# Taking GpSimd's tensor work in the mixing stages of a two-layer hybrid kernel over to VectorE and ScalarE

## The chip, the cores and the metric

The kernel runs on one core of a Trainium2 chip. The number that counts is the device time of one execution in microseconds (us). Three runs of the kernel before gave 1757.34, 1757.70 and 1763.57 us; their median is 1757.7 us.

A core has TensorE (PE in the profile, with its weight loads as PEld), VectorE (DVE), ScalarE (ACT), GpSimd (POOL) and SyncE (SP), which here only issues DMAs. Each engine works through its own queue in order; semaphores make one wait for another.

## The reference

Two layers work on 512 latent tokens and 256 context tokens of width 1024, all in float32. A layer mixes the tokens and then runs a gated MLP:

```python
mix_c, finals = token_mixers(modulate(cs, csh1, csc1), None, lw, want_out=not last, want_finals=True)
mix_x, _ = token_mixers(modulate(xs, sh1, sc1), finals, lw, want_out=True, want_finals=False)
xs = layer_norm(DEEPNORM_ALPHA * xs + g1 * mix_x, ln1_g[l], ln1_b[l])
ffn_x = conv_ffn(modulate(xs, sh2, sc2), ffn_w_up[l], ffn_conv_w[l], ffn_conv_b[l], ffn_w_down[l], rows)
xs = layer_norm(DEEPNORM_ALPHA * xs + g2 * ffn_x, ln2_g[l], ln2_b[l])
# token_mixers: proj = h @ w_in, and two groups on its columns
#   S5:  32 groups x 64 complex states, scanned forwards and backwards; y = Re(C states) + D u; gelu; glu
#   LRU: conv of 4, gates r, i; a = exp(-8 r softplus(-lam)); h = scan(a, sqrt(1-a^2) i x); (h_fwd + h_bwd) * gelu(g)
#   out = concat(y_s5, y_lru) @ w_out
```

The context tokens go through the same layers, except that the second layer needs only their final states.

## The kernel before

**Split products.** Every large matrix product is made of three passes at a reduced-precision format (`mm3`, lines 170 to 172). For it each operand is split into a high part and a low part: `split` (lines 158 to 163) writes `hi` as a rounded copy and `lo = src - hi`. `halves` (line 195) loads a piece of weights of 128 x 1024 into one of two staging buffers (`r0`, `r1`), and splits it; a staging buffer is free again when the low part is done. The high part is made by ScalarE (line 160), or, for `w_in` of the second layer, by GpSimd (line 162; `HIE = 'SG'`). The low part of all weights is made by GpSimd (line 163).

**Stages.** Each layer has a mixing stage and an FFN stage.

The mixing stage projects the normalised tokens with 12 column blocks of `w_in` (`proj`): u (S5 input), x (LRU input), g (LRU gate), four each. S5 works through eight head blocks `hb` of four groups. For each, `prep` gets two tables `ein` and `fo` (in the first layer from `outer`, lines 595 to 600, with `fo` on GpSimd and `ein` on VectorE; in the second from DRAM), transposes one, and makes a table of the products inside a block of 8 tokens. `enter` multiplies the inputs into states, copies them to SBUF and sets up `rt`, a broadcast of the decay (line 709, GpSimd). `leave` rotates by a table `cs` (lines 722 to 725), scans (line 727, twice), rotates back (731 to 738), multiplies out on TensorE (741 to 743), and ScalarE evicts the result (744). The rotation tables themselves come from `s5_params` (lines 575 to 577): for each `hb` three instructions on GpSimd for the cosine part, three on VectorE for the sine part. The first layer's are made inside its own mixing stage, the second layer's during the first layer's FFN stage. The LRU (`__call__`) makes gates with TensorE and ScalarE (783, 784), decays (794, 795, 803), scans on VectorE (804 to 812), and adds the two directions on GpSimd (line 813). After the last `hb`, `glu` loads the S5 result back from DRAM (961), applies gelu (965), splits it, multiplies by `w_glu`, gates it with a sigmoid (976, 977), and splits again; the LRU result, times its gelu gate (935), is split under the name `ylru` with its low part on GpSimd. Then come the products with `w_out`, the normalisation and the next features.

In the FFN stage (lines 1141 to 1180) TensorE runs nearly without a gap, VectorE does the convolution and GpSimd the low parts of the weights.

**Order.** The program is written in the order of its text, with priorities and filler work (matrix products for the modulation, `mods`) given in tables such as `FILL`; a scheduler with a timeline of its own then sets the order on each engine. Moving an instruction to another engine so changes the order of others as well.

Of the kernel before, what the change touches and what calls it, by code (L numbers as in the profile page):

```python
# [17 lines left out]
AF = mybir.ActivationFunctionType  # L18
ALU = mybir.AluOpType
MUL, ADD, SUB = ALU.mult, ALU.add, ALU.subtract  # L20
# [17 lines left out]
PI_LO = 3.1415925  # L38
PRIO = (300, 300)
PRIO2 = (0, 0)  # L40
HIE = 'SG'
VG = (1,)
PRIO3 = (0, 0)
MODS = (2, 1)
# [8 lines left out]
def body(ctx: ExitStack, tc: tile.TileContext, a, out):  # L53
    nc = tc.nc
    V, S, G, PE = nc.vector, nc.scalar, nc.gpsimd, nc.tensor
# [54 lines left out]
    def new(slot, shape, dt=F32):  # L110
        t, o, has = slots[slot]
        assert has == dt, (slot, dt)
        return carve(t, o, shape)
# [39 lines left out]
    V.memset(mhalf, -0.5)  # L153
    

    hi_eng = [None]

    def split(src, hi, lo, lo_eng):
        if hi_eng[0] is None:
            S.activation(hi, src, AF.Copy)  # L160
        else:
            hi_eng[0].tensor_scalar(hi, src, 1.0, None, op0=MUL)  # L162
        return lo_eng.tensor_tensor(lo, src, hi.bitcast(F32), op=SUB)  # L163
# [32 lines left out]
    def halves(src, hi, lo):  # L196

        raw = raws(hi.shape)
        with behind(hold[0]):
            weight_load[0] = load(raw, src)  # L200
        split(raw, hi, lo, G)
        return hi, lo


# [237 lines left out]
    def s5_params(l, scratch, raw_slots, phase_slots, cs_slots, tmp_slot, load=load):  # L442
# [27 lines left out]
        r8 = prm["r8"]  # L470
# [94 lines left out]
        for hb in range(8):  # L565
            yield
            step()
            gs = slice(4 * hb, 4 * hb + 4)
            cs = new(cs_slots[hb % 2], [128, 2, 4, 96])
            tt = new(tmp_slot, [128, 2, 4, 96])  # L570
            bh = lambda i: hi[:, i, gs].unsqueeze(3).to_broadcast([128, 4, 12, 8])
            bl = lambda i: lo[:, i, gs].unsqueeze(2).to_broadcast([128, 4, 12, 8])
            w = lambda x: x.rearrange("p g (a b) -> p g a b", b=8)
            for i, e, op in ((0, G, SUB), (1, V, ADD)):
                e.tensor_tensor(w(cs[:, i]), bh(0), bl(i), op=MUL)
                e.tensor_tensor(w(tt[:, i]), bh(1), bl(1 - i), op=MUL)
                e.tensor_tensor(cs[:, i], cs[:, i], tt[:, i], op=op)
            nc.sync.dma_start(csd[l, hb], cs.rearrange("p i g n -> p (i g n)"))
# [41 lines left out]
    class S5:  # L620
# [29 lines left out]
        def prep(self, hb):  # L650
# [4 lines left out]
            fo2 = fo.rearrange("p i g j c -> p i g (j c)")  # L655
            ein = new("a0", [128, 2, 4, 8, 16])
            if l == 0:
                outer(fo, hb, 2, prm["cc"], False, G, self.tg)
                outer(ein, hb, 0, prm["bb"], True, V, self.tv)
            else:  # L660
                load(ein.rearrange("p i g j c -> p (i g j c)"), tabd[hb, 0])
                load(fo.rearrange("p i g j c -> p (i g j c)"), tabd[hb, 1])
# [30 lines left out]
        def enter(self, hb, et):  # L693
# [12 lines left out]
            self.copy(v[0:64, :, :, 1:96], vv[0:64, :, :, 0:95])  # L706
            self.copy(v[64:128, :, :, 1:33], vv[64:128, :, :, 31::-1])
            self.copy(v[64:128, :, :, 33:96], vv[64:128, :, :, 95:32:-1])
            G.tensor_scalar(rt, self.prm["r8"][:, gs].unsqueeze(2).to_broadcast([128, 4, 96]), 1.0, None, op0=MUL)
            G.memset(rt[:, :, 0:1], 0.0)  # L710
            cs = new("t0", [128, 2, 4, 96])
            load(cs.rearrange("p i g n -> p (i g n)"), csd[self.l, hb])
# [34 lines left out]
    class LRU:  # L747
# [23 lines left out]
        def __call__(self, m, xc, bank):  # L771
# [33 lines left out]
            for d in range(2):  # L805
# [4 lines left out]
                    V.tensor_tensor_scan(h[:, 0:LAT], aa[:, 0:LAT], i_[:, 0:LAT], h[:, NT - 1:NT], op0=MUL, op1=ADD)  # L810
                else:
                    V.tensor_tensor_scan(h[:, ::-1], aa[:, ::-1], i_[:, ::-1], 0.0, op0=MUL, op1=ADD)
            G.tensor_tensor(hs[0][:, 0:keep], hs[0][:, 0:keep], hs[1][:, 0:keep], op=ADD)
            return hs[0]

    tmps = ring("gr", "gs")
# [53 lines left out]
    for l in range(DEPTH):  # L870
# [2 lines left out]
        ntok = 128 * nt  # L873
        order = order0[6 - nt:]
        cols, coef = par[l]
        if l > 0:
            mixing_phase()

# [142 lines left out]
        where[0] = f"ylru{l}"  # L1021
        ylru = [[new(f"h{2 * m + i}", [128, NT], F32R) for i in range(2)] for m in range(4)]
        for m in range(4):
            split(ge[0][:, m, 0:ntok], ylru[m][0][:, 0:ntok], ylru[m][1][:, 0:ntok], G)

        ys5 = y5s[0]
        phase("right", (F32R, several("x", 6, 4)), (F32R, {"w6": 4, "w7": 4}))
        where[0] = f"out{l}"
        gt = new("v", [128, 2, D])
        g1 = [bcast(gt[:, v], gd[l][0, v]) for v in range(1 if last else 2)]  # L1030
        xin = [new("u", [128, 3, D]), new("e", [128, 3, D])]
# [270 lines left out]
```

## Time and profile before

| | us |
|---|---|
| median of three runs | 1757.7 |
| the profiled execution | 1757.56 |
| its span, first to last instruction | 1755.8 |
| PE busy | 1562.5 (89%) |
| DVE busy | 1302.9 (74%) |
| POOL busy | 807.7 (46%) |
| ACT busy | 648.1 (37%) |

The stages can be told apart in the page's 40 slices of 43.9 us each: the first layer's mixing takes slices 1 to 8 and its FFN stage ends in the 23rd or 24th; the second layer's mixing ends in the 30th. An engine's busy time is the sum of the times from its instructions' starts to their ends, so a duration is read beside that of the same shape elsewhere. The stretch from 43.3 us (the modulation factors of the first features are done) to 299.7 us (the last S5 scan of the first layer ends) is called the head below, and that from there to 366.0 us (the last gate product of `glu`) the tail.

### The profile page before, as it was taken

What the parts mean: (1) busy time and instruction counts of PE and PEld (TensorE: products, weight loads), DVE (VectorE), ACT (ScalarE), POOL (GpSimd) and SP (SyncE); (2) the same over time, 40 slices, a digit from 0 to 9 for tenths busy, and PEclk for the clock granted to TensorE, in tenths of its full rate; (3) what the DMA queues carried; (4) which work ended last, traced back from release to release, by engine and by line L of the source; (5) the groups of instructions that cost most, each with busy time, mean ns of one, the idle gap of its engine ahead of it and who ended that gap; (6) DMA issues with size and microseconds to landing.
All of it is one profiled execution on the core that took longest, in us unless ns stands there. A gap on an engine that the chain in (4) does not pass through costs nothing. (4 is left out here: it accounts for less than half of the span.)

```text
span 1755.8 us, 22958 instructions
## 1 busy us (share of the span) xinstructions
PE 1562.5 (89%) x8824; PEld 1267.1 (72%) x8824; DVE 1302.9 (74%) x2104; ACT 648.1 (37%) x941; POOL 807.7 (46%) x496
## 2 busy tenths in 40 slices
PE   4768778898999999999999779989869899999996
PEld 1656655677888787887888658767547888888884
DVE  7999999478566995677689883889557476555587
ACT  2426445633633222222222136344661643323320
POOL 2567543548332244522325383533156454444474
PEclk8788898999899999999999898998879899999998
DMA  8335435742221212423334315665463333232231
GB/s 332 105 114 162 136 113 185 231 154 92 78 72 61 96 49 97 156 109 131 118 118 150 111 52 185 212 213 171 152 209 125 102 120 108 84 108 96 85 120 60
DMA packets 95359, 227.10 MB, mean 129 GB/s; under 512 B 28912, under 2 KB 39696, under 8 KB 95248
## 3 DMA queue, kind: packets, MB, share of 16 engines
q1 hardware_dynamic: 85456, 212.92, 36.3%
q10 hardware_dynamic: 9792, 12.71, 2.0%
q8 instruction: 69, 1.13, 0.3%
q14 instruction: 42, 0.34, 0.1%
HBM read 194.50 MB, written 31.10 MB: 128 GB/s over the span
## 5 line engine op out<-in xcount | busy, mean ns | idle before, releaser
L170 PE MATMUL banks<-ar,ar 128*128 128x512 f32 (+2 forms) x2152 | 777.6, 367 | 49.1 <-ACT ar L160 16.8
L171 PE MATMUL banks<-ar,ar 128*128 128x512 f32 (+2 forms) x2152 | 778.3, 363 | 17.3 <-DVE ar L396 7.8
L172 PE MATMUL banks<-ar,ar 128*128 128x512 f32 (+2 forms) x2152 | 770.9, 362 | 2.3 <-DVE ar L163 2.2
L163 POOL TENSOR_TENSOR ar<-ar,ar 128x1024 fp32r<-128x1024 f32 (+1 forms) x184 | 456.0, 2485 | 572.2 <-ACT ar L160 479.5
L170 PEld LDWEIGHTS banks<-ar,ar 128*128 128x128 f32 x2152 | 412.8, 193 | 134.0 <-ACT ar L160 20.8
L171 PEld LDWEIGHTS banks<-ar,ar 128*128 128x128 f32 x2152 | 415.7, 193 | 82.9 <-DVE ar L396 9.7
L172 PEld LDWEIGHTS banks<-ar,ar 128*128 128x128 f32 x2152 | 415.5, 193 | 65.7 <-DVE ar L163 4.2
L160 ACT ACTIVATE ar<-ar 128x1024 fp32r<-128x1024 f32 (+3 forms) x236 | 226.1, 976 | 496.7 <-PE banks L171 202.1
L1141 DVE SCALAR_TENSOR_TENSOR ar<-banks,cols,ar 128x441 f32<-128x441 f32 (+2 forms) x352 | 243.1, 691 | 41.8 <-ACT ar L1136 35.0
L1175 DVE TENSOR_TENSOR ar<-banks,ar 128x512 f32<-128x512 f32 x160 | 109.0, 685 | 117.4 <-PE banks L172 115.4
L163 DVE TENSOR_TENSOR ar<-ar,ar 128x512 fp32r<-128x512 f32 (+1 forms) x64 | 77.8, 1228 | 56.0 <-ACT ar L160 39.1
L826 POOL TENSOR_TENSOR ar<-ar 128x512 f32<-128x512 f32 x40 | 62.2, 1560 | 47.8 <-DVE ar L822 47.1
L1148 ACT ACTIVATE ar<-ar,cols 128x768 f32<-128x768 f32 (+1 forms) x44 | 36.6, 831 | 122.2 <-DVE ar L1141 71.4
L185 PE MATMUL banks<-ar,cond 128*32 128x256 f32 x192 | 64.8, 441 | 18.9 <-DMA ar<-in_w_mod_dram 18.9
L384 PE MATMUL banks<-ident,ar 128*128 128x128 f32 x176 | 36.5, 345 | 34.4 <-ACT ar L358 16.4
L188 PE MATMUL banks<-ar,cond 128*32 128x256 f32 x576 | 65.8, 441 | 0.0
L396 DVE TENSOR_TENSOR ar<-ar,ar 128x256 fp32r<-128x256 f32 (+1 forms) x64 | 41.4, 666 | 32.9 <-ACT ar L395 32.6
L783 PE MATMUL banks<-ar,ar 128*128 128x512 f32 (+1 forms) x128 | 54.7, 550 | 7.8 <-issue 6.9
L162 POOL TENSOR_SCALAR ar<-ar 128x1024 fp32r<-128x1024 f32 x12 | 35.5, 2958 | 49.2 <-PE banks L171 27.5
L384 PEld LDWEIGHTS banks<-ident,ar 128*128 128x128 f32 x176 | 26.2, 175 | 41.5 <-ACT ar L358 17.4
L1136 ACT ACTIVATE ar<-banks,cols 128x512 f32<-128x512 f32 x44 | 29.9, 679 | 69.7 <-PE banks L172 69.6
L185 PEld LDWEIGHTS banks<-ar,cond 128*32 128x32 f32 x192 | 15.8, 115 | 54.8 <-DMA ar<-in_w_mod_dram 32.4
(255 smaller groups left out, 1921.0 us busy)
## 6 DMA issues: line engine op xcount, KB each, us to landing
ar<-in_w_mod_dram SPq DMA_DIRECT2D x96, 512.0 KB
ar<-in_ffn_w_up_dram SPq DMA_DIRECT2D x88, 512.0 KB
ar<-in_ffn_w_down_dram SPq DMA_DIRECT2D x44, 512.0 KB
ar<-in_w_in_dram SPq DMA_DIRECT2D x24, 512.0 KB
tabd<-ar SPq DMA_DIRECT2D x16, 512.0 KB
ar<-tabd SPq DMA_DIRECT2D x16, 512.0 KB
csd<-ar SPq DMA_DIRECT2D x16, 384.0 KB
ar<-csd SPq DMA_DIRECT2D x16, 384.0 KB
```

The source lines that it names most:

```text
L160: S.activation(hi, src, AF.Copy)
L163: return lo_eng.tensor_tensor(lo, src, hi.bitcast(F32), op=SUB)
L170: PE.matmul(ps, wh, xh, start=first and k == 0, stop=False)
L171: PE.matmul(ps, wh, xl, start=False, stop=False)
L172: PE.matmul(ps, wl, xh, start=False, stop=last and k == nk - 1)
L185: ins = PE.matmul(*args, **kw)
L188: ins = PE.matmul(*args, **kw)
L384: PE.transpose(tp[:, o:o + 128], z[:, 128 * k:128 * k + 128], ident)
L783: PE.matmul(gp, w[:, d, i, :], xc[:, o:o + n], start=True, stop=True)
L826: G.tensor_tensor(xs_t[:, cs], xs_t[:, cs], tmp, op=ADD)
L1141: inst[0] = V.scalar_tensor_tensor(av[:, yo, xo], uv[:, yi, xi], tap(1 + dy, 1 + dx, ch), av[:, yo, xo], op0=MUL, op1=ADD)
L1175: V.tensor_tensor(acc, ps, acc, op=ADD)
```

## The change

`HIE` becomes `'SS'`: ScalarE makes the high parts of `w_in` in both layers. A variable `lo_eng` says who makes the low parts of weights: VectorE in the mixing stages (`w_in`, `w_glu`), GpSimd from the output product on (`w_out` and the FFN weights), as before. VectorE also takes the cosine half of the rotation tables of both layers, the table `fo` of the first layer, the sum of the two LRU directions and the low part of `ylru`; ScalarE takes the broadcast `rt`. What is left to GpSimd in the mixing stages are memsets and the small steps of the normalisation.

```diff
-HIE = 'SG'
+HIE = 'SS'
...
-    hi_eng = [None]
+    hi_eng, lo_eng = [None], [V]
...
             weight_load[0] = load(raw, src)
-        split(raw, hi, lo, G)
+        split(raw, hi, lo, lo_eng[0])
         return hi, lo
...
-            for i, e, op in ((0, G, SUB), (1, V, ADD)):
+            for i, e, op in ((0, V, SUB), (1, V, ADD)):
                 e.tensor_tensor(w(cs[:, i]), bh(0), bl(i), op=MUL)
...
             if l == 0:
-                outer(fo, hb, 2, prm["cc"], False, G, self.tg)
+                outer(fo, hb, 2, prm["cc"], False, V, self.tg)
                 outer(ein, hb, 0, prm["bb"], True, V, self.tv)
...
-            G.tensor_scalar(rt, self.prm["r8"][:, gs].unsqueeze(2).to_broadcast([128, 4, 96]), 1.0, None, op0=MUL)
+            S.activation(rt, self.prm["r8"][:, gs].unsqueeze(2).to_broadcast([128, 4, 96]), AF.Copy)
...
-            G.tensor_tensor(hs[0][:, 0:keep], hs[0][:, 0:keep], hs[1][:, 0:keep], op=ADD)
+            V.tensor_tensor(hs[0][:, 0:keep], hs[0][:, 0:keep], hs[1][:, 0:keep], op=ADD)
...
         cols, coef = par[l]
+        lo_eng[0] = V
         if l > 0:
             mixing_phase()
...
         for m in range(4):
-            split(ge[0][:, m, 0:ntok], ylru[m][0][:, 0:ntok], ylru[m][1][:, 0:ntok], G)
+            split(ge[0][:, m, 0:ntok], ylru[m][0][:, 0:ntok], ylru[m][1][:, 0:ntok], V)
...
         where[0] = f"out{l}"
+        lo_eng[0] = G
         gt = new("v", [128, 2, D])
```

In all, 140 instructions come to VectorE: 36 low parts (line 163: 24 of `w_in`, 4 of `w_glu`, 8 of `ylru`), 48 of lines 575 to 577, 48 of lines 595 to 600 and 8 of line 813; 28 come to ScalarE: 12 high parts and 16 of line 709. From line 876 on the new text's line numbers are one higher, from line 1023 on two.

The scheduler's order changes in three places that matter here. The first is VectorE at the end of the first layer's mixing. Before, after the last scan (727) and its rotation back, the last LRU part (798 and on) begins:

```order
L727 SCALAR_TENSOR_TENSOR ar_68<-ar_68 128x384 x2
L731 TENSOR_TENSOR ar_68<-ar_68 128x768
L732 TENSOR_TENSOR ar_68<-ar_68 128x768
L735 TENSOR_TENSOR ar_68<-ar_68 64x384
L737 TENSOR_TENSOR ar_68<-ar_68 64x4x32
L738 TENSOR_TENSOR ar_68<-ar_68 64x4x64
L735 TENSOR_TENSOR ar_68<-ar_68 64x384
L737 TENSOR_TENSOR ar_68<-ar_68 64x4x32
L738 TENSOR_TENSOR ar_68<-ar_68 64x4x64
L798 TENSOR_TENSOR ar_83<-ar_83,ar_87 128x768
```

Now the last LRU part (its scans 812 and 810, its sum 813), the last low part of `w_in` and the gate (936, line 935 before) stand ahead of that scan:

```order
L812 SCALAR_TENSOR_TENSOR ar_89<-ar_84,ar_85 128x768
L810 SCALAR_TENSOR_TENSOR ar_88<-ar_82,ar_88,ar_83 128x512
L722 TENSOR_TENSOR ar_68<-ar_68 128x768
L723 TENSOR_TENSOR ar_68<-ar_68 128x768
L813 TENSOR_TENSOR ar_88<-ar_88,ar_89 128x768
L163 TENSOR_TENSOR ar_67<-ar_68,ar_67 128x1024
L724 TENSOR_TENSOR ar_68<-ar_68 128x384
L725 TENSOR_TENSOR ar_68<-ar_68 128x384
L936 TENSOR_TENSOR ar_68<-ar_68,ar_80 128x768
L727 SCALAR_TENSOR_TENSOR ar_68<-ar_68 128x384 x2
L731 TENSOR_TENSOR ar_68<-ar_68 128x768
L732 TENSOR_TENSOR ar_68<-ar_68 128x768
```

So the whole last LRU part moved from behind the last S5 block to ahead of its scan.

The second place is ScalarE there, around the eviction of the last S5 block (744) and its store to DRAM (648). Before, they follow the last decay of the LRU (803) at once:

```order
L803 ACTIVATE ar_88<-ar_88,lru_st_2068 128x768
L803 ACTIVATE ar_89<-ar_89,lru_st_2068 128x768
L744 ACTIVATE ar_68<-banks 128x384
L648 DMA yd<-ar_68 128x768
L924 ACT_TABLE_LOAD
L924 ACTIVATE ar_68<-banks 128x512
```

Now the high parts of `ylru` (160, 128x768) and three of `w_out` (160, 128x1024 into `ar_66`) stand ahead of them:

```order
L160 ACTIVATE ar_66<-ar_68 128x768 x3
L160 ACTIVATE ar_66<-ar_68 128x1024 x2
L927 ACTIVATE ar_68<-banks 128x256
L160 ACTIVATE ar_66<-ar_68 128x768
L160 ACTIVATE ar_66<-ar_68 128x1024
L744 ACTIVATE ar_68<-banks 128x384
L648 DMA yd<-ar_68 128x768
```

The eviction moved behind other work of ScalarE, while the LRU's decays moved out of its way.

The third is GpSimd between the layers. Before, high and low parts of the second layer's `w_in` (162, 163) stand between the steps of the last normalisation (352, 366, 367), the residual sums (826) and the low parts of features (396):

```order
L396 TENSOR_TENSOR ar_66<-ar_68,ar_66 128x256
L162 TENSOR_SCALAR ar_67<-ar_68 128x1024
L826 TENSOR_TENSOR ar_68<-ar_68 128x512
L352 TENSOR_TENSOR ln_st_7506<-ln_st_7506,mhalf_98 128x1
L366 TENSOR_TENSOR ln_st_7467<-ln_st_7467,mhalf_98 128x1
L162 TENSOR_SCALAR ar_67<-ar_68 128x1024
L163 TENSOR_TENSOR ar_67<-ar_68,ar_67 128x1024
L704 MEMSET ar_68 128x8
L826 TENSOR_TENSOR ar_68<-ar_68 128x512
L704 MEMSET ar_68 128x8
L396 TENSOR_TENSOR ar_66<-ar_68,ar_66 128x256
```

Now none do:

```order
L396 TENSOR_TENSOR ar_66<-ar_68,ar_66 128x256
L826 TENSOR_TENSOR ar_68<-ar_68 128x512
L366 TENSOR_TENSOR ln_st_7467<-ln_st_7467,mhalf_98 128x1
L352 TENSOR_TENSOR ln_st_7506<-ln_st_7506,mhalf_98 128x1
L367 TENSOR_TENSOR ln_st_7467<-ln_st_7467 128x1
L704 MEMSET ar_68 128x8
L826 TENSOR_TENSOR ar_68<-ar_68 128x512
L704 MEMSET ar_68 128x8
L639 MEMSET ar_68 128x256
L396 TENSOR_TENSOR ar_66<-ar_68,ar_66 128x256
```

Three instructions of 128x1024 have left GpSimd's queue between these two steps of the features.

## Rows read from the trace of the kernel before

**Rows 1.** The page's 40 slices: busy tenths of DVE.

```profile
DVE  7999999478566995677689883889557476555587
```

**Rows 2.** By stretch: length; PE, PEld, DVE, ACT, POOL busy (count); PEclk; DMA; GB/s.

```profile
43.30:299.70 256.40, 195.76 (x1354) 154.91 (x1354) 249.85 (x374) 118.20 (x191) 149.14 (x105) 0.84 0.42 133
299.70:366.00 66.30, 57.00 (x341) 43.06 (x341) 39.81 (x37) 42.64 (x59) 32.00 (x13) 0.95 0.65 215
...
500.00:1006.00 506.00, 487.27 (x2637) 409.15 (x2635) 394.49 (x715) 125.39 (x153) 186.25 (x94) 0.99 0.31 106
1006.00:1066.00 60.00, 48.52 (x200) 37.61 (x201) 43.36 (x76) 26.28 (x49) 44.73 (x43) 0.81 0.26 95
1066.00:1255.00 189.00, 171.90 (x1314) 138.39 (x1313) 143.07 (x193) 88.28 (x149) 70.94 (x45) 0.91 0.61 192
1255.00:1316.00 61.00, 45.56 (x271) 31.35 (x270) 28.88 (x25) 39.70 (x54) 28.43 (x14) 0.80 0.54 177
```

**Rows 3.** Timeline, all engines, 83 to 91.5 us: start, duration, instruction, [idle before].

```profile
83.39 2.39 POOL L163 TENSOR_TENSOR ar<-ar,ar 128x1024 fp32r<-128x1024 f32 x1 [5.90 <-ACT ar L160]
83.44 2.50 DVE L261 TENSOR_TENSOR ar<-ar,ar 128x128 f32<-128x128 f32 x1
...
90.93 0.28 DVE L261 TENSOR_TENSOR ar<-ar,ar 128x128 f32<-128x128 f32 x1
```

**Rows 4.** DVE's groups by line and shape in the head: count, busy us, mean ns.

```profile
L723 DVE TENSOR_TENSOR ar<-ar 128x768 f32<-128x768 f32 x8 | 11.9, 1483 | 0.0
...
L597 DVE TENSOR_TENSOR ar<-ar,ar 128x512 f32<-128x512 f32 x8 | 9.3, 1168 | 0.0
...
L804 DVE SCALAR_TENSOR_TENSOR ar<-ar,ar 128x768 f32<-128x768 f32 x6 | 5.6, 938 | 0.0
L599 DVE TENSOR_TENSOR ar<-tab,bb 128x512 f32<-128x512 f32 x8 | 5.4, 678 | 0.0
```

**Rows 5.** POOL's groups by line and shape in the head.

```profile
L163 POOL TENSOR_TENSOR ar<-ar,ar 128x1024 fp32r<-128x1024 f32 x13 | 34.6, 2660 | 28.5 <-ACT ar L160 28.5
...
L709 POOL TENSOR_SCALAR ar<-r 128x384 f32<-128x384 f32 x7 | 14.1, 2021 | 23.0 <-DVE ar L727 23.0
```

**Rows 6.** Timeline of DVE, SP and ACT at the tail, 296 to 366 us.

```profile
296.60 0.54 DVE L724 TENSOR_TENSOR ar<-ar 128x384 f32<-128x384 f32 x1
297.07 0.55 DVE L725 TENSOR_TENSOR ar<-ar 128x384 f32<-128x384 f32 x1
...
303.61 0.42 DVE L738 TENSOR_TENSOR ar<-ar 64x256 f32<-64x256 f32 x1
...
313.09 0.47 ACT L744 ACTIVATE ar<-banks 128x384 f32<-128x384 f32 x1
...
324.34 0.20 ACT L963 ACTIVATE glu_st<-ar 128x1 f32<-128x1 f32 x1 [6.22 <-DMA ar<-yd]
...
339.85 3.15 DVE L163 TENSOR_TENSOR ar<-ar,ar 128x768 fp32r<-128x768 f32 x1
...
358.11 7.01 DVE L163 TENSOR_TENSOR ar<-ar,ar 128x512 fp32r<-128x512 f32 x6 [0.21 <-ACT ar L160]
```

**Rows 7.** Timeline between the layers, 1040 to 1056 us, all engines.

```profile
1046.06 2.77 POOL L162 TENSOR_SCALAR ar<-ar 128x1024 fp32r<-128x1024 f32 x1
...
1048.81 2.34 POOL L163 TENSOR_TENSOR ar<-ar,ar 128x1024 fp32r<-128x1024 f32 x1
...
1053.19 0.58 PE L171 MATMUL banks<-ar,ar 128*128 128x256 f32 x1 [6.11 <-POOL ar L396]
...
1053.49 1.28 DVE L830 SCALAR_TENSOR_TENSOR ar<-ar,ln_st 128x1024 f32<-128x1024 f32 x1
```

**Rows 8.** The whole run's groups by line and shape: ScalarE's high parts.

```profile
L160 ACT ACTIVATE ar<-ar 128x1024 fp32r<-128x1024 f32 x164 | 173.7, 1060 | 399.9 <-PE banks L171 139.4 <-DMA ar<-in_ffn_w_up_dram 96.2 <-PE banks L172 87.4
```

**Rows 9.** Timeline at the end of the second layer's mixing, 1284 to 1300 us.

```profile
1288.36 7.22 DVE L163 TENSOR_TENSOR ar<-ar,ar 128x512 fp32r<-128x512 f32 x3
...
1291.18 0.58 PE L171 MATMUL banks<-ar,ar 128*128 128x256 f32 x1 [2.17 <-DVE ar L163]
```

## The prediction

> **What bounds the kernel now.** I read the page's slices first. VectorE is at nine tenths or more in slices 2 to 7, that is, through the first layer's mixing, and again in a few slices of the FFN [rows 1]. The stretches then say what each stage hangs on [rows 2]. In the head (43.3 to 299.7 us) VectorE is busy 249.85 of 256.40 us, while TensorE is busy 195.76 and its clock stands at 0.84 of full, so part of it at the lower of its two levels (1.2 instead of 2.4 GHz): there VectorE is the bound. In the FFN stage (500 to 1006) TensorE is busy 487.27 of 506 us at 0.99. In the second layer's mixing (1066 to 1255) TensorE is busy 171.90 of 189 us, VectorE 143.07. Between them (1006 to 1066), in the tail (299.7 to 366) and at the end of the second mixing (1255 to 1316), nobody is full: chains of waits set the time.
>
> The timeline shows what VectorE's busy time is made of [rows 3]. GpSimd began a low part of 128x1024 at 83.39 and took 2.39 us; VectorE's product of 128x128, begun at 83.44, ended with it after 2.50 us. The same product took 0.28 us at 90.93. An instruction of VectorE with two operands in SBUF so stands until GpSimd is done. By lines and shapes [rows 4]: 128x768 takes 938 ns where it is undisturbed (line 804) and 1483 in the mean at line 723, which makes 8 x 0.545 = 4.4 us of waiting; 128x512 takes 678 (599) and 1168 (597), 3.9 us. The same subtraction over all 83 groups of VectorE in the head gives 79 us. GpSimd is busy 149.14 us there [rows 2], and it stands as well.
>
> **The change part by part.** *Head.* The 79 us of waiting go, as GpSimd keeps only memsets. What comes: by the new order, 87 moved instructions lie between the first modulation factors and the last scan: 13 low parts at 1.28 us (128x1024 on VectorE with two SBUF operands, line 830 [rows 7]), 46 of lines 595 to 600 at 0.678, 24 of lines 575 to 577 at 0.55 [rows 6], 4 sums at 0.938: 16.6 + 31.2 + 13.2 + 3.8 = 64.8 us. The last LRU part, which the scheduler takes ahead of the last scan, adds ten instructions, about 10.2 us (seven of 128x768 and three scans), and three moved ones before 43.3 us add 2.6. VectorE starts an instruction before the one ahead of it has ended: 0.47 us apart where each takes 0.55 [rows 6]. For 100 instructions at 0.07 that takes 7 off. VectorE's time is then 249.85 - 79 + 64.8 + 10.2 + 2.6 - 7 = 241.4 us, with the idle 6.55 as before 248, against 256.4: -8. Its inputs must be ready as often as now, though it no longer falls behind while it stands; I take -5. The ends: -15 if its idle time goes too; +15 if line 709, for which GpSimd waited 23.0 us on the scan [rows 5], makes VectorE's inputs late by that much now that it stands in ScalarE's queue.
>
> *Tail.* In the chain the last S5 block is rotated back (line 738 ends at 304.03), but ScalarE evicts it only at 313.09, behind the decays of the last LRU part [rows 6]. These are done earlier now; ahead of the eviction stand instead the last piece of ylru (a low part, a gate, a high part, some 3 us) and high parts of w_out (1.06 each [rows 8]): about 4 us instead of 9, so -5; but if those wait for staging buffers that GpSimd frees at 2.66 us each [rows 5], two of them, it is 0. Then, behind the reload (324.34), low parts take 3.15 us for 0.938 (at 339.85) and 7.01 for six of 0.678, that is 4.1 (at 358.11) [rows 6]. The subtraction over the whole tail gives 13 us of waits; GpSimd's ylru work, which causes most, goes, its low parts of w_out stay. I count 5 of the 13: the sigmoids and products between them pace the rest. Tail: -10, between -17 and +5.
>
> *FFN stage of the first layer.* The 24 table instructions of the second layer make 24 x 0.55 = 13 us on VectorE, which is idle 506 - 394 = 111 us beside a full TensorE [rows 2]; GpSimd's share of the same goes. I take 0. Without that cover it would be +13, and if the shorter waits are felt, -5.
>
> *Between the layers.* GpSimd makes a high part (2.77 us at 1046.06) and a low part (2.34 at 1048.81) just ahead of a residual sum and the features that TensorE stands 6.11 us for [rows 7]. Both go: 5.1 us; ScalarE and VectorE have 1.06 and 1.28 us more each in queues that feed the same features. I take -4, between -6 and -1.
>
> *Second mixing.* 12 high parts at 1.06 and 8 of line 709 at about 0.5 (between 0.47, the eviction of 384 elements [rows 6], and 1.06) come to ScalarE, 17 us on 88 of 189. VectorE gets some 17 us of work and loses some 23 of waits, by the subtraction as above. TensorE sets the pace: -2, between -8 and, if all of ScalarE's is felt, +17. What is queued behind line 709 on ScalarE are evictions of the next block's transposes and gates, then high parts.
>
> *End of the second mixing.* Three low parts take 7.22 us for 3 x 0.678 = 2.0, and TensorE waits 2.17 on one [rows 9]. The ylru low parts and the LRU sum leave GpSimd, those of w_out stay: -3, between -5 and 0.
>
> *Sum.* -5 - 10 + 0 - 4 - 2 - 3 = -24. The profiled execution took 1757.56 us (span 1755.8 and 1.76 around it), and the median of the runs is 1757.7, so they agree: 1757.56 - 24 = 1733.6, say 1734 us.
>
> **The rivals.** *One queue instead of two.* VectorE's own work in the head, 249.85 - 79 = 171 us, and GpSimd's 149 make 320 us in 256: 64 us ran side by side, and now run in one line. If VectorE then falls to 90% busy, since each of its gaps is lost for good, the head takes 241.4 / 0.90 = 268 us, 12 longer, and the whole 1757.56 + 12 - 10 - 4 - 2 - 3 = 1751. For it: 0.97 of the time would have to be kept. Against it: at 0.97 VectorE was always behind, so its inputs lay ready. The Trainium skill speaks for this rival ("Perfetto Trace Analysis", section "Optimizing Scalar/DVE Operations"): GpSimd and VectorE share a read port, so moving work between the two might not help. By that rule the head would come out near its old length; the trace agrees on the standing still (2.50 for 0.28 us), but has the low part at half the time on VectorE (1.28 against 2.66), which is where I expect the gain.
>
> *ScalarE stands at line 709 (the slower side).* GpSimd could wait for the previous scan at no cost; ScalarE can't, since behind it in the same queue stand the evictions that free TensorE's banks. If the 23.0 us of waiting [rows 5] come in full, and as much again in the second layer with half of it felt beyond the 5 of slack I leave, the head is 23 - 5 = 18 longer, the second mixing 17, the tail gains nothing, the rest -7: 1757.56 + 28 = 1786. It decides where the mean wait at 709 passes some 3 us a block (23.0 over 7) with TensorE waiting at the same time. Against it: ScalarE is idle 138 of 256 us in the head, and the order puts 709 behind the evictions that belong to the earlier block.
>
> *The clock comes up.* Between the layers and at the end of the second mixing the granted clock averages 0.81 and 0.80 [rows 2], which is 2 x 0.19 x 60 = 23 and 2 x 0.20 x 61 = 24 us at 1.2 GHz, each after TensorE had stood. If the waits that go take all of that with them, 47 us of work take half: 23 us more, 1711.
>
> **How the numbers follow.** The forecast has 0.56, with its own range of 1722 to 1748. One queue has 0.17, ScalarE's stall 0.13, the clock 0.14. About 8.8 us (0.5%) is what a measurement of this kernel can tell from no change, so "the same" is 1749 to 1766. The forecast and the clock lie below it: faster 0.70; one queue inside: 0.17; the stall above: 0.13. For the range I go down to the clock's 1711 and up to where only the worse part of the stall is left out, 1763; the ends of all terms together (-56 and +49) would need every unknown to fall on one side.
>
> **What would show it.** Head: GpSimd nearly idle, lines 723 and 597 back at 0.94 and 0.68 us, VectorE still above 95%, the last scan (line 727, sixteenth) ending at 290 to 297 us. Tail: 744 within 5 us of the last 738, the low parts at undisturbed durations until w_out's begin, the last gate product 54 to 58 us behind the last scan instead of 66. FFN: TensorE's busy share unchanged. Between the layers: no wait of TensorE on features above 3 us. I am wrong if VectorE's busy share in the head falls below 0.92, if ScalarE waits more than 3 us a block at line 709, or if VectorE's durations do not fall once GpSimd rests.

## The result and the profile after

The changed kernel takes 1736.74 us (median of 4 runs, 1729.82 to 1738.61), the kernel before in the same comparison 1758.68 (4 runs, 1757.34 to 1763.57): a ratio of 0.9863, 95% interval 0.9829 to 0.9897. It is faster by 22 us (1.4%, clear of no change by its interval), where 24 were forecast. The profiled execution took 1738.61 us with a span of 1736.8, 19.0 us under the span of before.

By events, which each timeline shows (the end of the first modulation factors, of scans 727 and of gate products 977, which are line 978 after), the 19 us come from other places than forecast. The forecasts were made for the fixed stretches of [rows 2], so at the edges of the stages the two columns fit only roughly:

| stage, up to | before us | after us | difference | forecast |
|---|---|---|---|---|
| first modulation factors | 43.5 | 42.1 | -1.4 | in the head |
| head: sixteenth scan | 256.2 | 256.6 | +0.4 | -5 |
| tail: last gate product of `glu` | 66.3 | 60.8 | -5.5 | -10 |
| FFN: first product after TensorE's wait of 8.0 us at its end | 640.2 | 637.7 | -2.5 | 0 |
| between the layers: second scan of layer two | 101.4 | 96.6 | -4.8 | -4 |
| second mixing: last scan | 123.9 | 116.2 | -7.7 | -2 |
| its end: last gate product | 84.5 | 87.0 | +2.5 | -3 |
| the rest, to the end of the span | 439.8 | 439.8 | 0 | 0 |

The same stretches answer to [rows 2]; the first two are bounded by those events, the later ones only roughly (their bounds were moved along with the stages). Columns as there:

```profile
42.10:298.70 256.60, 220.47 (x1550) 172.13 (x1550) 239.52 (x471) 141.99 (x223) 1.41 (x13) 0.87 0.50 160
298.70:359.50 60.80, 30.91 (x144) 27.76 (x145) 29.28 (x27) 26.66 (x36) 22.22 (x9) 0.70 0.43 141
...
493.50:998.50 505.00, 487.80 (x2643) 409.63 (x2642) 406.90 (x741) 126.39 (x154) 155.25 (x68) 1.00 0.31 106
998.50:1053.00 54.50, 43.45 (x189) 33.99 (x189) 42.95 (x76) 26.77 (x47) 37.31 (x37) 0.88 0.30 102
1053.00:1235.00 182.00, 167.57 (x1325) 134.58 (x1324) 135.30 (x207) 102.60 (x171) 3.61 (x16) 0.95 0.63 200
1235.00:1297.00 62.00, 44.01 (x269) 31.24 (x267) 30.13 (x31) 39.82 (x54) 21.92 (x8) 0.81 0.53 183
```

In the head GpSimd is down to 1.41 us. VectorE does 97 instructions more in 10 us less busy time, but it is idle 17.1 us instead of 6.6, and the stretch is as long as before. The groups of VectorE in the head say that the standing is gone [rows 4]:

```profile
L723 DVE TENSOR_TENSOR ar<-ar 128x768 f32<-128x768 f32 x8 | 7.6, 953 | 0.0
...
L804 DVE SCALAR_TENSOR_TENSOR ar<-ar,ar 128x768 f32<-128x768 f32 x8 | 7.4, 953 | 6.0 <-ACT ar L803 6.0
...
L597 DVE TENSOR_TENSOR ar<-ar,ar 128x512 f32<-128x512 f32 x16 | 10.9, 689 | 0.0
```

Line 723 went from 1483 to 953 ns, line 597 from 1168 to 689. The largest piece of the new idle time stands at line 804: 6.0 us of waiting for ScalarE's decays. Another 5.1 us are waits for the rotation tables on their way through DRAM (2.9 at line 722, 2.2 at line 575), and 2.3 a wait for a gate of the LRU (798 on 784). Line 709, now ScalarE's, in the same stretch and in the second layer's mixing (two answers):

```profile
L709 ACT ACTIVATE ar<-r 128x384 f32<-128x384 f32 x7 | 3.6, 521 | 13.3 <-DVE ar L727 13.3
L709 ACT ACTIVATE ar<-r 128x384 f32<-128x384 f32 x7 | 3.6, 521 | 7.4 <-DVE ar L727 7.4
```

It waits 1.9 and 1.1 us a block, under the 3 us from which it was to decide.

The tail, in the timelines of VectorE, ScalarE and SP (start, duration, instruction, idle before), answers to [rows 6]:

```profile
298.71 0.96 DVE L731 TENSOR_TENSOR ar<-ar 128x768 f32<-128x768 f32 x1
299.59 3.10 DVE L732 TENSOR_TENSOR ar<-ar 128x768 f32<-128x768 f32 x1
302.61 3.96 DVE L163 TENSOR_TENSOR ar<-ar,ar 128x768 fp32r<-128x768 f32 x2
...
308.48 0.42 DVE L738 TENSOR_TENSOR ar<-ar 64x256 f32<-64x256 f32 x1
...
331.56 1.83 DVE L163 TENSOR_TENSOR ar<-ar,ar 128x768 fp32r<-128x768 f32 x2 [18.95 <-ACT ar L160]
...
310.79 1.80 ACT L160 ACTIVATE ar<-ar 128x768 fp32r<-128x768 f32 x2 [10.72 <-DVE ar L936]
313.56 0.49 ACT L744 ACTIVATE ar<-banks 128x384 f32<-128x384 f32 x1 [0.98 <-PE banks L743]
314.08 0.35 ACTq L648 DMA_DIRECT2D yd<-ar  x1
...
315.02 7.58 SPq L200 DMA_DIRECT2D ar<-in_w_out_lru_dram  x2
322.69 0.39 SPq L962 DMA_DIRECT2D ar<-yd  x1
```

GpSimd works here on low parts of `w_out` (two from 298.93 on, 5.95 us), and beside them line 732 takes 3.10 us for 0.95 and two low parts of `ylru` 3.96 for 1.8. They stand ahead of the last rotation back, so line 738 ends at 308.9, 10.2 us behind the last scan; before it was 4.3. The store of the S5 result takes 7.1 us: it goes out at 314.08, and the last of its DMA packets ends at 321.17. The reload (962) goes out 1.5 us later, since it stands in SP's queue behind two loads of `w_out`, the second of which waits until GpSimd's next low part (319.91 to 322.25) frees a staging buffer. So 7.1 of the 8.6 us from the store to the reload are the store's own. Until the result is back VectorE is idle 18.95 us.

### The profile page after: what moved, and what is told of

Same layout as the page of the kernel before. It is cut to its first block, busy times and chain, and to the rows that moved or that the text cites. A ratio compares the mean times of both kernels' runs of the same rounds, so it can differ in the third digit from the quotient of the medians.

```text
span 1736.8 us, 22939 instructions
## 1 busy us (share of the span) xinstructions
PE 1551.8 (89%) x8824; PEld 1263.5 (73%) x8824; DVE 1287.7 (74%) x2244; ACT 672.1 (39%) x972; POOL 522.7 (30%) x328
## 5 line engine op out<-in xcount | busy, mean ns | idle before, releaser
L163 POOL TENSOR_TENSOR ar<-ar,ar 128x1024 fp32r<-128x1024 f32 x148 | 364.9, 2473 | 672.8 <-ACT ar L160 596.1
L160 ACT ACTIVATE ar<-ar 128x1024 fp32r<-128x1024 f32 (+2 forms) x248 | 238.9, 981 | 488.4 <-PE banks L171 212.3
L1177 DVE TENSOR_TENSOR ar<-banks,ar 128x512 f32<-128x512 f32 x160 | 109.4, 687 | 106.5 <-PE banks L172 104.5
L163 DVE TENSOR_TENSOR ar<-ar,ar 128x512 fp32r<-128x512 f32 (+2 forms) x100 | 113.6, 1148 | 81.0 <-ACT ar L160 64.3
L783 PE MATMUL banks<-ar,ar 128*128 128x512 f32 (+1 forms) x128 | 55.5, 563 | 10.3 <-ACT ar L925 5.7
L396 DVE TENSOR_TENSOR ar<-ar,ar 128x256 fp32r<-128x256 f32 (+1 forms) x64 | 32.8, 531 | 31.8 <-ACT ar L395 31.7
L822 DVE TENSOR_TENSOR ar<-banks,ar 128x512 f32<-128x512 f32 x60 | 40.5, 681 | 18.7 <-PE banks L172 18.7
```

Of the source, the lines that this page charges most:

```text
L783: PE.matmul(gp, w[:, d, i, :], xc[:, o:o + n], start=True, stop=True)
L822: V.tensor_tensor(tmp, ps, g[:, cs], op=MUL)
L1177: V.tensor_tensor(acc, ps, acc, op=ADD)
```

## The experiments

All are compared with the kernel before on the same chip, whose median was 1756.1 to 1760.7 in these comparisons, so it is the ratios that are compared. The stages are taken by the events above (us); from the third column on: from the end of the tail to the second scan of layer two, on to its last scan, and on to its last gate product.

| kernel | head | tail | to 2nd scan | to last scan | to last gate | median | ratio (95%) |
|---|---|---|---|---|---|---|---|
| before | 256.2 | 66.3 | 741.6 | 123.9 | 84.5 | 1758.7 | 1 |
| changed | 256.6 | 60.8 | 734.3 | 116.2 | 87.0 | 1736.7 | 0.9863 (0.9829 to 0.9897) |
| high_on_gpsimd | 256.5 | 60.8 | 736.9 | 118.5 | 81.9 | 1739.7 | 0.9880 (0.9850 to 0.9910) |
| low_on_gpsimd | 266.4 | 61.2 | 734.1 | 119.9 | 85.2 | 1755.1 | 0.9971 (0.9956 to 0.9985) |
| tables_on_gpsimd | 250.3 | 61.4 | 735.7 | 114.5 | 85.9 | 1734.3 | 0.9848 (0.9821 to 0.9875) |
| wout_low_on_vectore | 255.0 | 56.1 | 730.9 | 116.8 | 86.7 | 1733.5 | 0.9838 (0.9810 to 0.9866) |
| low_alone | 249.1 | 65.5 | 734.7 | 118.0 | 86.2 | 1742.8 | 0.9907 (0.9875 to 0.9939) |
| decay_on_gpsimd | 263.6 | 61.0 | 733.5 | 115.8 | 79.2 | 1736.2 | 0.9866 (0.9835 to 0.9897) |
| sums_ylru_on_gpsimd | 261.8 | 60.4 | 732.3 | 118.4 | 83.0 | 1740.4 | 0.9891 (0.9864 to 0.9919) |
| tables_g_wout_v | 249.8 | 58.8 | 735.4 | 117.1 | 82.3 | 1727.2 | 0.9812 (0.9777 to 0.9847) |
| fo_g_wout_v | 243.5 | 57.2 | 733.9 | 116.3 | 82.2 | 1715.6 | 0.9748 (0.9724 to 0.9772) |
| tables_high_g_wout_v | 249.3 | 57.0 | 739.2 | 118.3 | 81.5 | 1732.2 | 0.9843 (0.9819 to 0.9868) |
| cosine_left_out | 262.5 | 56.2 | 732.4 | 114.1 | 85.4 | 1733.6 | 0.9856 (0.9826 to 0.9886) |
| last_lru_late | 254.6 | 58.4 | 735.7 | 117.4 | 86.0 | 1736.3 | 0.9878 (0.9851 to 0.9905) |

A stage's length comes from one profiled execution. In high_on_gpsimd, whose edit leaves the first layer alone, head and tail come out within 0.1 us of the changed kernel's. Each edit also lets the scheduler order the engines anew, so a row shows one part with the order that follows from it.

**The high parts.**

```diff
-HIE = 'SS'
+HIE = 'SG'
```

> The changed kernel with one part undone: the 12 high parts of the second layer's w_in are made by GpSimd again (HIE = 'SG'); all else as changed. Theory (GpSimd's slow copies stood in chains between the layers and made VectorE stand in the second mixing): 12 high parts of 2.8 to 3.0 us come back to GpSimd; TensorE's wait on the features between the layers returns by some 3 us, and the second mixing, which the change made 7.7 us shorter, loses half of that: 1744 us, first layer unchanged within 2 us. Rival (the gain there comes from the low parts, the decay broadcast and the sums instead): within 3 us of the changed kernel, 1737.

The theory's places were right (+2.6 to the second scan, +2.3 in the second mixing), the total was the rival's: the end of the second mixing is 5.1 us shorter than in the changed kernel. At that place TensorE's timeline of the changed kernel shows, among the products of `glu`:

```profile
1264.84 0.80 PE L170 MATMUL banks<-ar,ar 128*128 128x256 f32 x2 [3.72 <-ACT ar L160]
...
1276.73 0.40 PE L185 MATMUL banks<-ar,cond 128*32 128x256 f32 x1 [3.68 <-DMA ar<-in_w_mod_dram]
```

A modulation product stands ahead of the next products of `glu` in TensorE's queue and waits 3.68 us for its weights. With the high parts on GpSimd no such wait falls there: TensorE's waits for modulation weights in this stretch are 10.8 us in all in the changed kernel, 7.0 with the high parts on GpSimd and 6.9 in the kernel before. In this mix of parts the move of the high parts brought the total nothing that can be measured.

**The low parts.**

```diff
-    hi_eng, lo_eng = [None], [V]
+    hi_eng, lo_eng = [None], [G]
...
-        lo_eng[0] = V
+        lo_eng[0] = G
```

> The changed kernel with one part undone: the low parts of w_in and w_glu (28) are made by GpSimd again. Theory (standing next to GpSimd costs VectorE more than the work saves): 13 low parts leave VectorE in the head, 13 x 1.22 = 16 us, and some 20 to 30 us of standing come back: the head ends up to 10 us later; between the layers +2, second mixing +4, ends of the mixings +2 each: 1750 us. Rival (one queue: VectorE is the bound in the head, every instruction taken off it gains): head 10 us earlier, 1727 us.

1755.1: nearly all of the gain is gone (the execution in the table is the fastest of ten, 1749.1), and the head is 9.8 us longer, as the theory had it. The head's stretch, and GpSimd's low parts in it:

```profile
41.30:307.70 266.40, 221.85 (x1550) 170.33 (x1550) 247.35 (x459) 142.59 (x224) 37.86 (x28) 0.86 0.47 154
```

```profile
L163 POOL TENSOR_TENSOR ar<-ar,ar 128x1024 fp32r<-128x1024 f32 x14 | 37.6, 2689 | 88.4 <-ACT ar L160 80.9 <-PE banks L172 7.4
```

VectorE has 12 instructions fewer than in the changed kernel (459 for 471), 14.6 us at 1.22 each, and is busy 7.8 us longer. So 14 low parts on GpSimd made it stand 22.4 us, 1.6 each: more than the 1.22 that it takes to make one. The prediction's subtraction, done over all groups here, gives nearly the same: 26 us of standing in this head, 4 in the changed kernel's. Line 723 is undisturbed this time (953 ns); which instruction is hit depends on what VectorE happens to do beside a low part.

The same part alone, on the kernel before (its `split(raw, hi, lo, G)` with `lo_eng[0]`, VectorE in the mixing stages, GpSimd from `w_out` on):

> The kernel before with one part of the change alone: the low parts of w_in and w_glu are made by VectorE; high parts, tables, sums, ylru and line 709 stay with GpSimd. Theory (the low parts carry the gain: in the head each costs VectorE 1.22 us of work and saves 1.8 us of standing and a wait behind GpSimd's queue, worth 10 us there, and as much in the second mixing): 1742 us, with the head 5 to 10 us shorter than before's 256.2. Rival (the gain is there only when GpSimd is empty, since any tensor work left on it makes VectorE stand): 1755 us.

1742.8, the theory's number, 17.9 us below its before (1760.7): most of the change's gain, with the head 7.1 us shorter than before although GpSimd keeps all the rest. So the rival is out: the low parts gain beside a working GpSimd too, and removing them and adding them alone agree.

**The tables.**

```diff
-            for i, e, op in ((0, V, SUB), (1, V, ADD)):
+            for i, e, op in ((0, G, SUB), (1, V, ADD)):
...
-                outer(fo, hb, 2, prm["cc"], False, V, self.tg)
+                outer(fo, hb, 2, prm["cc"], False, G, self.tg)
```

> The changed kernel with one part undone: the cosine halves of the rotation tables (48) and the table fo of the first layer (48) are made by GpSimd again. In the head 24 x 0.55 + 46 x 0.69 = 45 us of work leave VectorE. Theory (the exchange in the head is about even, since GpSimd's 90 us on these tables make VectorE stand about half of that time): the head's end moves by less than 6 us either way, 1737 us. Rival 1 (VectorE's own work bounds the head): the head 20 us shorter, 1717 us. Rival 2 (standing outweighs): the head 12 us longer, 1749 us.

The total can't be told from the changed kernel's; the head is 6.3 us shorter, just beyond what the theory allowed and far from 20. Its stretch:

```profile
42.90:293.20 250.30, 201.68 (x1405) 157.01 (x1406) 241.87 (x389) 126.76 (x204) 109.26 (x82) 0.85 0.45 145
```

VectorE is as busy (241.87 for 239.52) with 82 instructions fewer, 70 of them tables, the rest of the last LRU part, which falls behind the last scan again: for the tables standing and work are about even (by the subtraction the standing rises from 4 to 53 us, by 49, for the 45 us of table work that leave). What differs is idle time, 8.4 us for 17.1. In the head the move of the tables so gave back about what the low parts had won (6.3 and 7.1 us).

**The low parts of `w_out`.**

```diff
         where[0] = f"out{l}"
-        lo_eng[0] = G
...
         where[0] = f"ffn{l}"
+        lo_eng[0] = G
```

> The changed kernel with one part added: the low parts of w_out (8 a layer) go to VectorE as well; GpSimd makes low parts from the FFN on only. In the tail of the first layer VectorE stands beside them now: 3.10 us for 0.95 (line 732), 3.96 for 1.9, 5.57 for 1.9 (line 163), some 8 us on the way to the last gate product, and it is idle for 19 us between. Theory (standing is what keeps the tail long): 3 to 4 us less in each layer, 1730 us. Rival (the tail hangs on the store and reload of the S5 result and on ScalarE's order): within 3 us of the changed kernel, 1737.

The total, 1733.5, can't be told from the changed kernel's. The first layer's tail is 4.7 us shorter, near the theory; the second layer's end is not (86.7 for 87.0). Line 732 and the low parts there are undisturbed, and the reload still stands in SP's queue behind the loads of `w_out`:

```profile
298.46 0.95 DVE L732 TENSOR_TENSOR ar<-ar 128x768 f32<-128x768 f32 x1
299.33 1.82 DVE L163 TENSOR_TENSOR ar<-ar,ar 128x768 fp32r<-128x768 f32 x2
...
303.05 0.42 DVE L738 TENSOR_TENSOR ar<-ar 64x256 f32<-64x256 f32 x1
...
315.39 3.75 SPq L200 DMA_DIRECT2D ar<-in_w_out_lru_dram  x2
319.19 0.43 SPq L962 DMA_DIRECT2D ar<-yd  x1
```

The last rotation back ends 5.9 us behind the last scan instead of 10.2, and these 4.3 us are nearly all of the gain: from the eviction (744) to the last gate product it takes 45.8 us as against 45.9, although the standing further on is gone as well. The store's last packet ends at 315.28 here, but the reload goes out only at 319.19. The two loads ahead of it wait for staging buffers that VectorE's low parts free, so part of this tail is the order of SP's queue; no run moved the reload ahead of them.

**Line 709, and the sums with `ylru`.**

```diff
-            S.activation(rt, self.prm["r8"][:, gs].unsqueeze(2).to_broadcast([128, 4, 96]), AF.Copy)
+            G.tensor_scalar(rt, self.prm["r8"][:, gs].unsqueeze(2).to_broadcast([128, 4, 96]), 1.0, None, op0=MUL)
```

> The changed kernel with one part undone: the broadcast of line 709 goes back to GpSimd. In the head ScalarE stands 13.3 us in all at its seven instructions of line 709 behind the scan (727), and VectorE's 17 us of idle time there hold 8.2 us on ScalarE's gates and decays (lines 784 and 803). Theory (that standing makes VectorE idle): the head 4 us shorter, 1733 us. Rival (ScalarE has room, and the idle time comes from something else, such as the order of the last LRU part): head within 2 us, 1737 us.

The total is the rival's (1736.2), but the head is 7 us longer, which neither had, and the end of the second mixing as much shorter. VectorE is idle 22.3 us in that head (263.5 less 241.2) instead of 17.1. So the total shows no cost of ScalarE's standing at line 709; the run can't tell it from the new order that came with the edit.

```diff
-            V.tensor_tensor(hs[0][:, 0:keep], hs[0][:, 0:keep], hs[1][:, 0:keep], op=ADD)
+            G.tensor_tensor(hs[0][:, 0:keep], hs[0][:, 0:keep], hs[1][:, 0:keep], op=ADD)
...
-            split(ge[0][:, m, 0:ntok], ylru[m][0][:, 0:ntok], ylru[m][1][:, 0:ntok], V)
+            split(ge[0][:, m, 0:ntok], ylru[m][0][:, 0:ntok], ylru[m][1][:, 0:ntok], G)
```

> The changed kernel with one part undone: the sum of the two LRU directions (8) and the low parts of ylru (8) go back to GpSimd. Theory (in the tail the ylru low parts on VectorE stand ahead of the last rotation back, so that 738 ends 5 us later after the scan than before; but on GpSimd they make VectorE stand as well): about even, tail within 3 us, 1737 us. Rival 1 (the place in VectorE's queue is what costs): tail 4 us shorter, 1731 with both layers. Rival 2 (standing and GpSimd's 2 us durations cost more): tail 5 us longer, 1745.

1740.4, between the theory and the second rival. The 5 us lie in the head, not in the tail: the low parts of `ylru` now run on GpSimd just ahead of the last scan, and VectorE stands beside them there, at the scan itself for 3.2 us (two scans take 1.81 in the changed kernel):

```profile
299.29 4.97 DVE L727 TENSOR_TENSOR_SCAN ar<-ar 128x384 f32<-128x384 f32 x2
```

That is the second rival's mechanism at another place. In the total this run and the last are inconclusive, as their intervals overlap with the changed kernel's.

**Together.** Tables back on GpSimd, low parts of `w_out` on VectorE:

> The changed kernel with the tables (cosine halves and fo) back on GpSimd and the low parts of w_out on VectorE too. Theory (two independent gains, in the head -6.3 us and in the tail -4.7 us, as each gave alone against the changed kernel): head 250, tail 56 us, 1729 us in the median of runs, below both kernels. Rival (the two share one cause, VectorE's queue at the end of the head, and don't add): 1734 us.

1727.2: the theory, though not as a plain sum (head and tail 308.6, where 306.4 would be one). Then of the tables `fo` alone on GpSimd (`outer(fo, ..., G, ...)`, the cosine halves on VectorE):

> The changed kernel with the low parts of w_out on VectorE too and only the table fo of the first layer back on GpSimd; the cosine halves stay on VectorE. An instruction of fo on GpSimd made VectorE stand 0.80 us in the run with the tables on GpSimd and is 0.69 us of VectorE's work; one of the cosine halves 0.47 and 0.55. Theory (the price is standing against work, so fo belongs on VectorE and the cosines on GpSimd): this is the worse half, 1732 us, between the kernel with w_out's low parts alone moved (1733.5) and the one with all tables back (1727.2). Rival (what the tables cost on VectorE is idle time, since fo's 46 instructions lengthen the queue in which the scans stand): fo is the larger part, 1728 us.

Both were wrong by more than 12 us: 1715.6, the fastest of all. Some 6 us of the step from 1727.2 lie in the head (243.5 for 249.8), and there VectorE is busy 235.9 us instead of 241.9: with the cosine halves on VectorE it has 12 us more work of its own, and by the subtraction 16 us less of standing. And the kernel with all tables on GpSimd, plus `HIE = 'SG'`:

> The kernel with the tables on GpSimd and the low parts of w_out on VectorE, and the 12 high parts of the second layer's w_in on GpSimd as well. Theory (the high parts cost 4.4 us between the layers and in the second mixing, but its end hangs on the LRU's gates on ScalarE, so that an earlier S5 end is given back there): within 3 us of 1727.2. Rival (nothing is given back once the tail of the second mixing is freed of GpSimd): 4 us more, 1731.

1732.2, the rival's number: here the high parts are felt (+3.8 to the second scan), though the intervals overlap a little.

**Is VectorE's work the length of the head?**

```diff
-            for i, e, op in ((0, V, SUB), (1, V, ADD)):
+            G.memset(cs[:, 0], 1.0)
+            for i, e, op in ((1, V, ADD),):
```

> The changed kernel without the products of the cosine halves of the rotation tables in both layers (48 instructions on VectorE, 24 in the head: 13.3 us there); GpSimd fills that half with a constant instead, so the rotations differ. Theory (VectorE's own work sets the length of the head): the head, the tail with it, shorter by 10 to 13 us, 1725 us. Rival (VectorE's idle time of 17 us grows in return, because ScalarE's gates and decays and the tables' way through DRAM are late next): 5 us or less, 1732.

The total is the rival's, but the run doesn't decide the question, since VectorE is not busy any less with it. Only 2.5 of GpSimd's 14.15 us in this head are the fills. Another 10.3 are four low parts of `w_out`, which the new order puts ahead of the last scan, and four of VectorE's instructions stand 2.0 to 2.2 us each beside them there. So VectorE is busy 241.3 us in the head, where the changed kernel has 239.5, and idle 21.2 instead of 17.1; head and tail take 318.7 us instead of 317.4. The stretches of this kernel, and of `fo_g_wout_v` below it:

```profile
41.90:304.40 262.50, 217.75 (x1548) 169.44 (x1548) 241.31 (x453) 147.93 (x229) 14.15 (x23) 0.86 0.52 168
304.40:360.60 56.20, 31.02 (x146) 28.32 (x147) 22.98 (x23) 21.86 (x30) 11.59 (x5) 0.69 0.29 98
```

```profile
42.20:285.70 243.50, 191.76 (x1404) 152.21 (x1404) 235.91 (x412) 124.90 (x199) 71.56 (x58) 0.86 0.48 155
285.70:342.90 57.20, 53.96 (x299) 42.68 (x291) 40.54 (x50) 44.10 (x60) 0.00 (x0) 0.97 0.60 188
```

In head and tail together VectorE is busy 264.3 us here and idle 54.4; in the changed kernel 268.8 and 48.6; in `fo_g_wout_v` 276.5 and 24.3. The fastest is the busiest of the three: among them the length goes with the idle time. It is no rule for all: the kernel before was idle only 33 us in head and tail, and took 322.7, since 92 us of VectorE's busy time were standing (79 and 13 in the prediction's count). TensorE shows the other side of the idle time. It does 1550 and 144 matmuls in head and tail of the changed kernel, 1404 and 299 in `fo_g_wout_v`: in the one the LRU's work is done ahead of the last scan, and the tail has too little to do while the S5 result goes through DRAM.

**The order of the last LRU part.** In the changed kernel's table of the text's order, first layer (l3 is the last LRU part, g a gate block, s `glu`):

```diff
-FILL = ('u1 x0 u2 u3|l0 x1||g0 l1 x2 g1|l2 x3|l3|g2|g3 s', 'x0 u1 u2 u3|l0 x1|g0 l1|x2 g1|l2 x3||l3|g3 g2 s')
+FILL = ('u1 x0 u2 u3|l0 x1||g0 l1 x2 g1|l2 x3||g2|g3 l3 s', 'x0 u1 u2 u3|l0 x1|g0 l1|x2 g1|l2 x3||l3|g3 g2 s')
```

> The changed kernel with the same engines; only the text's order is changed: in the first layer the last LRU part is written after the last gate block instead of before the third, so that on VectorE it stands behind the last S5 scan again, as before the change. Theory (the head's gain went into pulling ten instructions of that LRU part, 10 us, ahead of the last S5 scan, after which VectorE stands idle for 19 us while the S5 result goes through DRAM): last scan 6 to 10 us earlier, its idle wait filled by the LRU part, the sum of head and tail 7 us shorter than the changed kernel's 317.4, and 1729 us. Rival (the order has no part in it; the tables on VectorE are what holds the S5 chain back): sum of head and tail within 3 us, 1736.

Head and tail take 313.0 us, 4.4 less: between the two, and the total can't be told from the changed kernel's. The last rotation back (738) ends at 300.7 instead of 308.9, but ScalarE evicts its product at 312.88, hardly earlier than the 313.56 of the changed kernel (timelines of VectorE, TensorE and ScalarE, and the wait on VectorE):

```profile
292.48 3.90 DVE L727 TENSOR_TENSOR_SCAN ar<-ar 128x384 f32<-128x384 f32 x2
...
304.67 0.71 PE L741 MATMUL banks<-ar,ar 128*128 128x96 f32 x2 [14.20 <-DMA ar<-td]
...
310.24 2.74 ACT L160 ACTIVATE ar<-ar 128x768 fp32r<-128x768 f32 x3 [8.21 <-DVE ar L936]
312.88 0.47 ACT L744 ACTIVATE ar<-banks 128x384 f32<-128x384 f32 x1
...
328.36 3.56 DVE L163 TENSOR_TENSOR ar<-ar,ar 128x768 fp32r<-128x768 f32 x4 [16.29 <-ACT ar L160]
```

Three things kept the rest of the gain. Low parts of `w_out` run on GpSimd ahead of the last scan here, and four of VectorE's instructions stand beside them for 2.1 to 2.2 us each, the scan among them (3.90 us for 1.81). The products of the last block (741) start only at 304.67, 4 us behind 738: they wait for the table of products inside a block on its way through DRAM (`td`), whose last step on VectorE (684) now stands behind the scan, at 298.15; in the changed kernel it ran at 287.85, ahead of it. The products end at 310.1, but the high parts of `ylru` stand ahead of the eviction in ScalarE's queue and wait for the gate (936), which is now nearly the last thing that VectorE does ahead of the reload: 2.8 us more. So the place of the LRU part in VectorE's queue was a part of it, and the order of the other work took most of the gain back.

## Why the prediction was right, point by point

- **That the standing goes.** Right: lines 723 and 597 fell to 953 and 689 ns, and the run with the low parts back showed the price, 1.6 us of standing for 1.22 of work.
- **Head.** VectorE's busy time was forecast as 248 less 6.6 of idle time, 241.4, and is 239.5. The count held: by the same subtraction 75 of the 79 us of standing went, the work rose by 75 us as counted, and the overlap gave 11 us instead of 7; only the 2.6 us counted for the stretch ahead of 43.3 us did not come, as the first modulation factors were done 1.4 us earlier. The step that failed is "with the idle 6.55 as before": it rose to 17.1 us, so the busy share fell to 0.933, short of the 0.95 named, and the last scan ended at 298.7 instead of 290 to 297. The waits that came are for ScalarE's decays (6.0 us), the tables from DRAM (5.1) and a gate (2.3). The low parts alone did give 7 us there. The rival of one queue named this mechanism (gaps are lost), with a share of 0.90 and 12 us more; the runs show 0.93 and 0.4 us more.
- **Tail.** Half as much as forecast. From the last scan to 738 it became 5.9 us longer, from there to the eviction (744) 4.4 shorter, to the first gate product 3.9 and to the last 3.0 shorter. So the forecast's two terms, -5 for the eviction and -5 for the low parts behind it, came out at -4.4 and -6.9. The eviction does follow 738 within 5 us (308.9 to 313.56), as forecast; the last gate product comes 60.8 us behind the scan where 54 to 58 were named. The mis-sized term is what was left out of the sum, the way to 738: the low parts of `ylru` in VectorE's queue and the standing beside `w_out`'s. Moving `w_out`'s to VectorE took 4.3 of these 5.9 us away, so most of it was the standing.
- **FFN.** 0 forecast, -2.5 measured, inside -5 to +13; TensorE's busy time is the same, 487.80 us, and covers the tables.
- **Between the layers.** -4 forecast, -4.8 measured. TensorE's two waits on features are now 3.56 and 3.28 us instead of 6.11 and 1.15: the long one is not below the 3 us named, and together they are 6.84 us instead of 7.26. So the number came out, but not by the shorter wait that was to give it. That GpSimd's high parts matter here is shown by the run that put them back: one wait of 7.42 us, and the second scan 2.6 us later. In the same stretch the granted clock was 0.88 instead of 0.81; what that gave was not taken apart.
- **Second mixing and its end.** -2 and -3 forecast, -7.7 and +2.5 measured. The granted clock came up with it, 0.95 instead of 0.91 [rows 2], and TensorE's busy time fell by 4.3 us for as many products: a part of what the rival on the clock had; at the end it hardly rose, 0.81 for 0.80. The end gave its gain back: TensorE's waits for modulation weights grew there from 6.9 to 10.8 us.
- **The rivals.** ScalarE waited 1.9 and 1.1 us a block at line 709, under the 3 that were to decide, and the total shows no cost of it. "One queue" was right that the head gains nothing (256.6 for 256.2), wrong by 11 us on its length, and wrong on the total, since the rest carried it. The rule of the Trainium skill ("Perfetto Trace Analysis", section "Optimizing Scalar/DVE Operations"), that moving work between GpSimd and VectorE might not help, fits the tables (49 us of standing against 45 of work) and does not fit the low parts, which alone shortened the head by 7.1 us.

That the sum came within 3 us of the measured median is in part luck, since misses of both signs cancelled: the first layer gave 9 us instead of 15, the second 10 instead of 9, and four terms (head with the first modulation factors, tail, second mixing, its end) were off by 4.0 to 5.7 us.

What stays open: why `fo` on GpSimd with the cosines on VectorE is 12 us better than all the tables there (half of it lies in the head, in less standing; the rest is spread over the stages), and why the head is 7 us longer with line 709 on GpSimd. The order changes with each of these edits. The one run that changed the text's order alone gained 4 us in head and tail, and nothing in the total that can be measured.

## What to carry to other kernels

Before moving work from GpSimd to VectorE, price each group by what its presence on GpSimd makes VectorE stand, not by its length: here a low part cost 1.6 us of standing for 1.22 us of work and was worth moving, while the tables as a whole were about even and were not. Then look at where the freed time goes: here into waits of VectorE on other engines, and into work pulled ahead of the last scan, while VectorE was idle for 19 us behind it. And try the parts apart, and halves of parts too: the best mix, which no expectation had, was 21 us below the whole change.

## What the runs showed of the hardware

VectorE's standing depends on where its operands are. In the FFN stage of the changed kernel GpSimd is busy 155 of 505 us, nearly all on low parts, and a group of VectorE with one operand in PSUM (`banks`) keeps its length, while one of the same size with both in SBUF does not:

```profile
L1177 DVE TENSOR_TENSOR ar<-banks,ar 128x512 f32<-128x512 f32 x96 | 65.3, 685 | 47.8 <-PE banks L172 47.7
...
L1182 DVE SCALAR_TENSOR_TENSOR ar<-ar 128x512 f32<-128x512 f32 x12 | 14.1, 1203 | 3.0 <-POOL ar L1181 3.0
```

Of the 96, twelve begin while GpSimd is at a low part, and they take 684 ns in the mean. Of the twelve with both operands in SBUF, two begin so, and take 2.30 and 2.88 us, where the shortest take 0.68.

The wait is until GpSimd's instruction ends, however small VectorE's own is. In the timeline, a step on 128x32 values, undisturbed and beside a low part:

```profile
561.30 0.18 DVE L232 SCALAR_TENSOR_TENSOR r<-r,ar 128x32 f32<-128x32 f32 x1
...
562.09 2.25 DVE L232 SCALAR_TENSOR_TENSOR r<-r,ar 128x32 f32<-128x32 f32 x1
```

GpSimd's low part ran from 561.90 to 564.30 there: 2.25 us for 0.18.
